# A two-layer hybrid decoder: attention values in column tiles, key blocks merged by the mask, gelu in one ScalarE function, and the last round's sums

## The chip, the cores and the metric

The kernel runs on one core of one Trainium2 chip. A core has five engines that run side by side, each in its own order: TensorE (PE, matrix products; its weight loads are shown as PEld), VectorE (DVE), ScalarE (ACT), GpSimd (POOL) and SyncE (SP, which issues DMAs). The metric is the device time of one execution in microseconds (us).

## What is computed

The input is x, 256 rows of 2048 float32 numbers; two layers are applied. The reference, cut to what matters here:

```python
for l in range(2):
    h = rms_norm(x, mix_norm[l])
    q, k, v, uv, gate_logits = split(h @ w_in[l])          # 16 q heads, 4 kv heads of 64
    q, k = rope(rms_norm(q)), rope(rms_norm(k))
    branch_a = sliding_window_attention(q, k, v, sinks[l]) @ w_attn_branch[l]
    branch_b = chunked_sgu(gelu(uv), w_spatial[l], ...) @ w_sgu_branch[l]
    gates = sigmoid(gate_logits)
    x = x + (gates[:, :D] * branch_a + gates[:, D:] * branch_b) @ w_out[l]
    h2 = rms_norm(x, ffn_norm[l])
    x = x + (silu(h2 @ w_gate[l]) * (h2 @ w_up[l])) @ w_down[l]
```

Attention works on blocks of 128 positions with a window of 128: a query sees the keys at its own position and at the 127 before it. In the first block these lie in that block alone. In the second block, query i sees the keys 0 to i of its own block and the keys i+1 to 127 of the block before: 128 keys in all. `gelu` is the form with tanh: x/2 times 1 + tanh(0.7978845608 (x + 0.044715 x^3)). The softmax has one more entry per head, the sink, which only adds to its denominator.

## The kernel before

**Products.** Each weight matrix streams from HBM in pieces of 256 rows by 512 columns (`raw`, 512 KB in float32; five buffers). Each piece is split into a high part (`whi`, ScalarE, L244) and a low part (`wlo`, VectorE, L245); the activations are split in the same way (`uh`, `ul`). `add_product` (L332 to L341) makes one product of a piece with 128 rows of activations out of six matmuls of 512 columns: high with high, high with low and low with high, for two halves of 128 weight rows. There are four buffers for split pieces; the split runs four pieces ahead of the product (`W_SPLIT`), the load seven (`W_LOAD`).

**Seven products for eight.** Where two column chunks share their activations (`pair`), the first 512 weight rows (unit `WINO`) are done by a Winograd-Strassen scheme with seven products (P1 to P7) for eight. It needs differences of weight pieces (`sums`, VectorE, L229) and of activations (`sums` at L499, split into `sh` and `sl` at L484 and L485). With `two=True` the second 512 rows are done so as well: one product less, three more weight splits and four more subtractions.

**Order.** PE's order is the order in which the program is written; the other engines are ordered by the compiler's schedule. Each two products advance a slot counter by one step (`tick`, L265 on). `after(n, fn)` puts work n steps later; what falls due in the same step is issued in the order in which it was put in. Each of a layer's stages goes through this list: the input projection in chunks (kv, q 0, q 1, gates, v, u), then the attention branch's projection, the SGU branch's, the output projection, then the gated feed-forward part in three rounds of 4, 4 and 3 chunks (`ROUNDS`), each followed by its part of `w_down` (`hid`).

**Attention.** A chunk c holds 8 query heads of two kv groups. `queries` (L722) puts `scores(t, g)` for block t and group g at steps 17, 22, 27, 32 after q 0 is there, and 29, 34, 39, 44 after q 1. `scores` (L745) makes 4 matmuls, two on rows 0 to 63 of the array and two on rows 64 to 127, of 128 columns for each key block, into two PSUM banks of the pool `at`, which has two (`ps_at`); it adds the mask, takes the maximum, Exp and the denominator. Five steps later `weights` (L778) transposes the probabilities of each key block on PE (bank pool `tr`, two banks) and copies them to `pT`; three steps later `values` (L789) multiplies: `pT` (128 x 128) is the stationary operand, 64 columns of v stream, 4 heads for each key block. VectorE divides by the denominator (`att`, L797). When a chunk is complete `transposed` turns `att` around: VectorE transposes blocks of 32 x 32, SP moves them with 16 DMAs, and ScalarE and VectorE split the result into `uh` and `ul`.

**Gelu.** `half` (L807) copies u or v out of PSUM with half the norm's scale. One and two steps later, for each 128 rows, `gelu` (L814) runs a Square and a Tanh on ScalarE and two operations on VectorE.

**Spatial weights.** `fetch` loads them on SP, POOL masks them; `spatial` (L648), 40 steps into the layer, transposes them on PE through both banks of `tr`, and VectorE copies them to `wsT`.

**Sums of the hidden units.** `hidden` (L976) hands `transposed` the steps `WINO_HID` (7, 8, 17, 18, 19, 20) for the first chunk of each round: two scaled copies, the split, the two halves of the sums, their split.

Of the kernel before, what the change touches and what calls it, by code (L numbers as in the profile page):

```python
# [38 lines left out]
WINO_HID = 7, 8, 17, 18, 19, 20  # L39
W_SPLIT = 4  # L40
# [7 lines left out]
Q_FIRST = 17  # L48
Q_STEP = 5
# [4 lines left out]
GELU_A = 0.044715  # L54
GELU_C = 0.7978845608028654
# [3 lines left out]
def hybrid_trunk(ctx: ExitStack, tc: tile.TileContext, x, mix_norm, w_in, q_norm, k_norm, sinks,  # L59
# [64 lines left out]

    def pair(key, wa, wb, by_unit=False, last_later=False, two=False):
# [34 lines left out]
    plans = []  # L160
    for l in range(DEPTH):
# [8 lines left out]
        plans += [single(("att", l), w) for w in cols_of(w_attn_branch[l], NCH)]  # L170
# [32 lines left out]
    class Stream:  # L203
# [7 lines left out]
        def load(self, upto):  # L211
            while self.asked < min(upto, len(entries)):
                for key, w, h, tag in entries[self.asked]["loads"]:
                    raw = (slot([P, 2, CW], name="raw") if tag == "slot" else
                           wraw.tile([P, 2, CW], F32, tag=tag, name=nm("raw"), bufs=None if tag == "raw" else 1))
                    src = w[2 * h * P:2 * (h + 1) * P, :].rearrange("(k p) n -> p k n", p=P)
                    if self.raws:
                        self.loaded = nc.sync.dma_start(raw, src)
                    else:
                        for i in range(2):  # L220
                            self.loaded = nc.sync.dma_start(raw[:, i:i + 1], src[:, i:i + 1])
                    self.raws[key] = raw
                self.asked += 1
# [330 lines left out]
    for c in range(NCH):  # L554
# [4 lines left out]
    mask = const.tile([P, S], F32, name="mask")  # L559
    nc.gpsimd.memset(mask, 0.0)  # L560
    nc.gpsimd.affine_select(mask[:, :P], mask[:, :P], pattern=[[1, P]], base=0, channel_multiplier=-1,
                            compare_op=ALU.is_gt, fill=-1e30)
    nc.gpsimd.affine_select(mask[:, P:], mask[:, P:], pattern=[[-1, P]], base=0, channel_multiplier=1,
                            compare_op=ALU.is_ge, fill=-1e30)
    cs = const.tile([P, NT, HD // 2], F32, name="cs")
# [97 lines left out]
    def fetch_large(pl):  # L663
        for n, i in ((13, 2), (17, 3), (21, 0), (25, 1)):
            after(n, lambda i=i: pl.fetch(i))
        after(40, pl.spatial)

    class Attention:


        def __init__(self, pl):
            self.pl = pl
            self.qT = [None] * 2
            self.att = [None] * 2
            self.attT = [None] * 2
            self.live = {}
# [38 lines left out]
        def keys(self, kv):  # L715
# [4 lines left out]
            after(K_TURN, lambda: turn(self.kT, kd.rearrange("p t n a d -> p t (n a d)"), nc.sync))  # L720

        def queries(self, c, q):  # L722
            self.rotate(q, NQ // 2, self.pl.rope[0], None)
            self.qT[c] = slot([P, 4, S], name="qT")
            self.att[c] = slot([P, NT, CW], name="att")
            after(Q_TURN, lambda: self.turn_queries(c, q))
            n = Q_FIRST + (4 * Q_STEP - 8) * c
# [17 lines left out]
        def scores(self, t, g):  # L745
            nk = P * (t + 1)
            mk = mask[:, P:] if t == 0 else mask
            snk, nsnk = self.pl.snk, self.pl.nsnk
            pr = slot([P, 2, 2, S], name="pr")
            for j in range(2):  # L750
                pscore = ps_at.tile([P, 2, S], F32, tag="at", name=nm("psc"))
                for i in range(2):
# [5 lines left out]
                nc.vector.tensor_tensor(out=pr[:, :, j, :nk], in0=pscore[:, :, :nk],  # L758
                                        in1=mk.unsqueeze(1).to_broadcast([P, 2, nk]), op=ALU.add)
            pr4 = pr.rearrange("p i j k -> p (i j) k")  # L760
            mx = tiny(4, "mx")
            nc.vector.tensor_reduce(out=mx, in_=pr4[:, :, :nk], axis=AX.X, op=ALU.max)
# [7 lines left out]
            for h in range(4):  # L770
                nc.scalar.activation(pr4[:, h, :nk], pr4[:, h, :nk], AF.Exp, bias=nm_[:, h:h + 1],
# [4 lines left out]
            after(5, lambda: self.weights(t, g, pr4, rd))  # L776

        def weights(self, t, g, pr4, rd):  # L778
            pT = []
            for kb in range(t + 1):  # L780
                pt = ps_tr.tile([P, 4, P], F32, tag="tr", name=nm("ppt"))
                for h in range(4):
                    nc.tensor.transpose(pt[:, h, :], pr4[:, h, kb * P:(kb + 1) * P], ident)  # L783
                pT_ = temp((P, 4, P), "pT")
                nc.scalar.activation(pT_, pt, AF.Copy)
                pT.append(pT_)
            after(3, lambda: self.values(t, g, pT, rd))

        def values(self, t, g, pT, rd):  # L789
            po = ps_at.tile([P, 4, HD], F32, tag="at", name=nm("po"))  # L790
            for h in range(4):
                for kb in range(t + 1):
                    nc.tensor.matmul(po[:, h, :], pT[kb][:, h, :],  # L793
                                     self.kv[:, kb, KVW + g * HD:KVW + (g + 1) * HD],
                                     start=kb == 0, stop=kb == t)
            o = (g % 2) * 256
            nc.vector.tensor_tensor(out=self.att[g // 2][:, t, o:o + 256].rearrange("p (h d) -> p h d", d=HD),  # L797
                                    in0=po, in1=rd.unsqueeze(2).to_broadcast([P, 4, HD]), op=ALU.mult)

    class Spatial:  # L800
# [6 lines left out]
        def half(self, ps, name):  # L807

            dst = slot([P, NT, CW], name=name)
            for t in range(NT):  # L810
                nc.scalar.activation(dst[:, t, :], ps[t], AF.Copy, scale=self.nrm.rh[t])
            return dst

        def gelu(self, dst, t):  # L814

            xh = dst[:, t, :]
            sq = temp(name="sq")
            nc.scalar.activation(sq, xh, AF.Square, scale=2.0)
            nc.vector.scalar_tensor_tensor(out=sq, in0=sq, scalar=1.0 / GELU_A, in1=xh,
                                           op0=ALU.add, op1=ALU.mult)  # L820
            nc.scalar.activation(sq, sq, AF.Tanh, scale=2.0 * GELU_C * GELU_A)
            nc.vector.scalar_tensor_tensor(out=xh, in0=sq, scalar=1.0, in1=xh, op0=ALU.add, op1=ALU.mult)

        def v(self, c, ps):
            self.vt[c] = vt = self.half(ps, "v")
            for t in range(NT):
                after(1 + t, lambda t=t: self.gelu(vt, t))
# [30 lines left out]
        def u(self, c, ps):  # L858
            ut = self.half(ps, "u")
            for t in range(NT):  # L860
                after(1 + t, lambda t=t: self.gelu(ut, t))
# [48 lines left out]
    for l in range(DEPTH):  # L910
# [65 lines left out]
        def hidden(hT, c):  # L976
# [6 lines left out]
            def on_up(up):  # L983
                for t in range(NT):
                    nc.vector.scalar_tensor_tensor(out=hid[:, t, :], in0=up[t], scalar=norm.r[t], in1=hid[:, t, :],
                                                   op0=ALU.mult, op1=ALU.mult)
                pe, soon = c == len(hT) - 1 == 2, c == 3
                after(3 if pe else 1 if soon else 2,
                      lambda: transposed(hT, c, hid, on_pe=pe, wino=WINO_HID if c == WINO else None,
# [53 lines left out]
```

## Time and profile before

| | |
|---|---|
| three runs | 2455.78, 2457.51, 2459.42 us; median 2457.51 |
| the profiled execution | 2457.45 us |
| its span, first to last instruction | 2455.7 us |
| mean granted TensorE clock | 0.999 of full speed |
| q1, the DMA queue of the weight loads | 486.35 MB, 61.0% of 16 engines' span |

A row of instructions by group reads: line of the kernel, engine, operation, what it writes <- what it reads, shape, x count | busy us in total, mean ns of one | idle time of the engine just before, and what ended it. A row of the timeline reads: start, duration, engine, line, operation, names, shape, x count, and in brackets the idle time before it and what ended it. The end of a matmul is modelled, so that matmuls in a row overlap in these rows; their starts tell the pace. A row of the waits reads: engine, what waited <- what it waited for: us in total, times, longest. A row of the windows reads: stretch in us, its length, then busy us (and instructions) of PE, PEld, DVE, ACT, POOL, then PE's granted clock, the DMA share and GB/s.

### The profile page before, as it was taken

The numbers are of one execution on the slowest core, as the hardware profiler recorded it, in microseconds if no ns is written. First come the engines' busy times: TensorE is split into PE (matmuls) and PEld (weight loads), VectorE is DVE, ScalarE is ACT, GpSimd is POOL, SyncE is SP. The second block draws the span as 40 slices with busy tenths as digits, with TensorE's granted clock in tenths as the row PEclk, the third lists the DMA queues.
The fourth block names the chain that finished last, engine by engine and source line by source line (L and its number), as shares of the span: only waits on it lengthen the run. The fifth ranks groups of instructions, "written<-read, shape, count | busy, mean of one in ns | idle before, by whom it ended". The sixth has DMA issues, their size and how long they took to land.

```text
span 2455.7 us, 31363 instructions
## 1 busy us (share of the span) xinstructions
PE 2438.1 (99%) x10968; PEld 2012.6 (82%) x10968; DVE 1999.5 (81%) x2320; ACT 1472.5 (60%) x1842; POOL 315.6 (13%) x592
## 2 busy tenths in 40 slices
PE   9999999999999999999999999999999999999999
PEld 7888888888888888887887888888888888888877
DVE  6798676797978997899877986768878789978996
ACT  5567544576655665566655665545666556655664
POOL 3100002132210111001101000021322101110110
PEclk9999999999999999999999999999999999999999
DMA  9555657576667657665747446675767675667654
GB/s 299 196 187 163 212 198 220 186 236 210 220 217 233 210 176 231 230 203 170 229 155 257 152 157 223 202 215 177 246 202 236 204 245 189 200 209 241 203 179 139
DMA packets 280782, 506.74 MB, mean 206 GB/s; under 512 B 28272, under 2 KB 40144, under 8 KB 280624
## 3 DMA queue, kind: packets, MB, share of 16 engines
q1 hardware_dynamic: 262544, 486.35, 61.0%
q0 software_dynamic: 17760, 18.12, 2.8%
q8 instruction: 86, 1.41, 0.2%
q14 instruction: 72, 0.59, 0.1%
q10 hardware_dynamic: 320, 0.27, 0.0%
HBM read 475.27 MB, written 2.10 MB: 194 GB/s over the span
## 4 chain that ended last, share of the span: by engine, by line
PE 90%; DVE 3%; DMA 3%; SPq 1%; issue 1%; ACT 1%; DVEq 0%; ACTq 0%
PE acc L340 59%; PE acc L341 29%; DMA raw<-in_w_in_dram 2%; DVE wlo L245 2%; SPq L416 1%; ACT whi L244 1%; PE po L793 1%; PE psc L754 0%; PE ppt L783 0%; DVE raw L229 0%; PE psg L871 0%; PE pt L453 0%; DMA raw<-in_w_up_dram 0%; DMA raw<-in_w_down_dram 0%; DVE box L410 0%
## 5 line engine op out<-in xcount | busy, mean ns | idle before, releaser
L244 ACT ACTIVATE whi<-raw 128x1024 fp32r<-128x1024 f32 (+1 forms) x1074 | 1132.0, 1059 | 883.0 <-PE acc L341 623.4
L245 DVE TENSOR_TENSOR wlo<-raw,whi 128x1024 fp32r<-128x1024 f32 (+1 forms) x1075 | 1301.3, 1219 | 399.0 <-ACT whi L244 386.7
L340 PE MATMUL acc<-whi,uh 128*128 128x512 f32 x2994 | 1170.3, 391 | 1.2 <-ACT uh L439 1.2
L340 PE MATMUL acc<-wlo,uh 128*128 128x512 f32 x2994 | 1167.1, 390 | 3.0 <-DVE wlo L245 2.9
L341 PE MATMUL acc<-whi,ul 128*128 128x512 f32 x2994 | 1166.4, 390 | 0.0
L340 PEld LDWEIGHTS acc<-wlo,uh 128*128 128x128 f32 x2994 | 562.6, 188 | 123.2 <-DVE wlo L245 6.0
L340 PEld LDWEIGHTS acc<-whi,uh 128*128 128x128 f32 x2994 | 562.6, 188 | 117.7 <-ACT uh L439 1.4
L341 PEld LDWEIGHTS acc<-whi,ul 128*128 128x128 f32 x2994 | 562.3, 188 | 117.8 <-DVE ul L444 0.5
L416 POOL DMA_DIRECT2D tt<-box x544 | 266.5, 497 | 1697.0 <-ACT whi L244 695.5
L229 DVE TENSOR_TENSOR raw<-raw,raw 128x1024 f32<-128x1024 f32 x236 | 287.8, 1219 | 1.6 <-DMA raw<-in_w_up_dram 0.8
L341 PE MATMUL acc<-whi,sl 128*128 128x512 f32 x472 | 184.0, 390 | 3.2 <-DVE sl L485 3.2
L340 PE MATMUL acc<-whi,sh 128*128 128x512 f32 x472 | 184.8, 392 | 1.7 <-ACT acc L364 1.7
L340 PE MATMUL acc<-wlo,sh 128*128 128x512 f32 x472 | 184.2, 390 | 0.0
L341 PEld LDWEIGHTS acc<-whi,sl 128*128 128x128 f32 x472 | 88.6, 188 | 22.5 <-DVE sl L485 4.0
L340 PEld LDWEIGHTS acc<-whi,sh 128*128 128x128 f32 x472 | 88.6, 188 | 20.9 <-ACT acc L364 2.1
L340 PEld LDWEIGHTS acc<-wlo,sh 128*128 128x128 f32 x472 | 88.7, 188 | 18.0
L366 DVE TENSOR_TENSOR kept<-acc,kept 128x512 f32<-128x512 f32 x94 | 64.3, 684 | 10.1 <-PE acc L341 10.1
L369 ACT ACTIVATE acc<-kept 128x512 f32<-128x512 f32 x94 | 54.9, 586 | 4.3 <-DVE kept L366 4.2
L888 DVE SCALAR_TENSOR_TENSOR xs<-acc,xs 128x512 f32<-128x512 f32 (+1 forms) x66 | 42.0, 668 | 8.4 <-PE acc L341 8.1
L436 DVE TENSOR_TENSOR ul<-tt,uh 128x512 fp32r<-128x512 f32 x52 | 34.0, 684 | 2.9 <-ACT uh L435 2.9
L435 ACT ACTIVATE uh<-tt 128x512 fp32r<-128x512 f32 x52 | 29.8, 618 | 9.4 <-DMA tt<-box 9.4
L312 POOL TENSOR_TENSOR rv<-ve,neg_half 128x4 f32<-128x4 f32 x8 | 11.9, 1486 | 172.9 <-DVE ve L839 159.5
(137 smaller groups left out, 874.8 us busy)
## 6 DMA issues: line engine op xcount, KB each, us to landing
raw<-in_w_in_dram SPq DMA_DIRECT2D x239, 512.0 KB, 4.7
raw<-in_w_gate_dram SPq DMA_DIRECT2D x176, 512.0 KB, 4.4
raw<-in_w_up_dram SPq DMA_DIRECT2D x176, 512.0 KB, 4.9
raw<-in_w_down_dram SPq DMA_DIRECT2D x176, 512.0 KB, 5.0
raw<-in_w_out_dram SPq DMA_DIRECT2D x64, 512.0 KB, 5.0
tt<-box POOLq DMA_DIRECT2D x544, 32.0 KB, 4.2
raw<-in_w_attn_branch_dram SPq DMA_DIRECT2D x32, 512.0 KB, 5.6
raw<-in_w_sgu_branch_dram SPq DMA_DIRECT2D x32, 512.0 KB, 4.4
```

The source lines that it names most:

```text
L229: self.last = nc.vector.tensor_tensor(out=self.raws[d], in0=self.raws[x], in1=self.raws[y], op=ALU.subtract)
L244: self.high = nc.scalar.activation(hi[:, i, :], raw[:, i, :], AF.Copy)
L245: self.last = nc.vector.tensor_tensor(out=lo[:, i, :], in0=raw[:, i, :], in1=hi[:, i, :].bitcast(F32), op=ALU.subtract)
L340: nc.tensor.matmul(ps, a, part[:, kk, :], start=first and kk + n == 0, stop=False, skip_group_check=True)
L341: nc.tensor.matmul(ps, b, hi[:, kk, :], start=False, stop=kk == 1, skip_group_check=True)
L366: nc.vector.tensor_tensor(out=p.kept[:, int(tag == "P7"), :], in0=a[1], in1=p.kept[:, 1, :], op=ALU.add)
L369: nc.scalar.activation(ps, p.kept[:, t, :], AF.Copy)
L416: q.dma_start(dst[j * B:(j + 1) * B, i], box[i * B:(i + 1) * B, j])
L435: nc.scalar.activation(h, s_, AF.Copy)
L436: nc.vector.tensor_tensor(out=l, in0=s_, in1=h.bitcast(F32), op=ALU.subtract)
L793: nc.tensor.matmul(po[:, h, :], pT[kb][:, h, :], self.kv[:, kb, KVW + g * HD:KVW + (g + 1) * HD], start=kb == 0, stop=kb == t)
L888: nc.vector.scalar_tensor_tensor(out=xs[:, t, sl], in0=sums[t][:, i * w:(i + 1) * w], scalar=scale, in1=xs[:, t, sl], op0=ALU.mult, op1=AL ...
```

## The change

1. **Key blocks merged.** For the second block the scores of both key blocks are still made. ScalarE copies those of the own block into `pr`; VectorE's `copy_predicated` overwrites those at k > i with the scores of the block before. Maximum, Exp and denominator then see 128 keys, not 256. `pr` is a 2 KB temporary now.
2. **Probabilities are normalised** (VectorE, 4 steps after the scores), then transposed 7 steps after the scores, one transpose for each head. For the second block VectorE makes a second copy with a causal factor (zero where k > i); v of block 0 is multiplied with the plain probabilities, and v of block 1 minus v of block 0 with the masked ones. That difference is made once a layer.
3. **Values.** v (128 x 64) is the stationary operand; the probabilities of 4 heads (512 columns) stream. The two kv groups of a chunk write partitions 0 to 63 and 64 to 127 of one bank: two column tiles of the array. The result has the layout of the activations' units, so `uh` and `ul` are made from the bank at once, and the transposes, DMAs and copies behind `att` go. Rows of `w_attn_branch` are loaded in the matching order, two DMAs of 64 partitions for each piece. `values(t, c)` runs 10 steps after the block's last scores.
4. **Gelu** is one ScalarE function from PSUM with the norm's scale, for each 128 rows.
5. **Spatial weights** are transposed at step 34, not 40.
6. **The last round's sums** (both layers) use `WINO_END`, 12 to 15 steps for the last four parts.
7. **The last pair** of the last `w_down` part in layer 1 runs with `two=True`, so its second hidden unit gets sums too.

```diff
+WINO_END = 7, 8, 12, 13, 14, 15
-Q_FIRST = 17
-Q_STEP = 5
+W_TURN = 7
+SCORES = (17, 22, 27, 32), (29, 34, 39, 44)
...
+    def rows_of(raw, w, h):
+        if w.shape[0] != QW or not any(w is a for a in by_heads):
+            return [(raw, w[2 * h * P:2 * (h + 1) * P, :].rearrange("(k p) n -> p k n", p=P))]
+        rows = w.rearrange("(c a k d) n -> c a d k n", c=2, a=2, d=HD)
+        k = 2 * (h % 2)
+        return [(raw[a * HD:(a + 1) * HD], rows[h // 2, a, :, k:k + 2]) for a in range(2)]
...
-            plans += [pair(("hid", l, r), c_[j], c_[j + 1], j == 0) for j in range(0, NCH, 2)]
+            plans += [pair(("hid", l, r), c_[j], c_[j + 1], j == 0, two=j > 0 and f1 == NF and l == DEPTH - 1)
+                      for j in range(0, NCH, 2)]
...
-        after(40, pl.spatial)
+        after(34, pl.spatial)
...
+            after(K_TURN, lambda: nc.vector.tensor_tensor(out=kv[:, 0, :KVW], in0=kv[:, 1, KVW:], in1=kv[:, 0, KVW:],
+                                                          op=ALU.subtract))
...
             for t in range(NT):
-                for g in (2 * c, 2 * c + 1):
-                    after(n, lambda t=t, g=g: self.scores(t, g))
-                    n += Q_STEP
-            after(n + 6, lambda: transposed(self.attT, c, self.att[c], queue=nc.sync))
+                for i in range(2):
+                    after(SCORES[c][2 * t + i], lambda t=t, g=2 * c + i: self.scores(t, g))
+                after(SCORES[c][2 * t + 1] + W_TURN + 3, lambda t=t: self.values(t, c))
...
-                nc.vector.tensor_tensor(out=pr[:, :, j, :nk], in0=pscore[:, :, :nk],
-                                        in1=mk.unsqueeze(1).to_broadcast([P, 2, nk]), op=ALU.add)
+                if t == 0:
+                    nc.vector.tensor_tensor(out=pr[:, :, j, :], in0=pscore[:, :, :P], in1=mk, op=ALU.add)
+                else:
+                    nc.scalar.activation(pr[:, :, j, :], pscore[:, :, P:], AF.Copy)
+                    nc.vector.copy_predicated(pr[:, :, j, :], mk.bitcast(mybir.dt.uint32), pscore[:, :, :P])
...
-            after(5, lambda: self.weights(t, g, pr4, rd))
+            after(4, lambda: nc.vector.tensor_tensor(out=pr4, in0=pr4, in1=rd.unsqueeze(2).to_broadcast([P, 4, P]),
+                                                     op=ALU.mult))
+            after(W_TURN, lambda: self.weights(t, g, pr4))
...
+            for h in range(4):
+                nc.tensor.transpose(pt[:, h, :], pr4[:, h, :], ident)
+            nc.scalar.activation(pT[0][:, g % 2], pt, AF.Copy)
+            if t == 1:
+                nc.vector.tensor_tensor(out=pT[1][:, g % 2], in0=pt, in1=causal.unsqueeze(1).to_broadcast([P, 4, P]),
+                                        op=ALU.mult)
+
+        def values(self, t, c):
...
+            po = ps_at.tile([P, 4, P], F32, tag="at", name=nm("po"))
+            pT = self.pT[t, c]
+            for k in range(t + 1):
+                for a in range(2):
+                    v = (1 - k) * KVW + (2 * c + a) * HD
+                    nc.tensor.matmul(po[a * HD:(a + 1) * HD], self.kv[:, 0, v:v + HD], pT[k][:, a],
+                                     start=k == 0, stop=k == t)
+            uh, ul = (x[:, :, t * P:(t + 1) * P] for x in units)
+            nc.scalar.activation(uh, po, AF.Copy)
+            nc.vector.tensor_tensor(out=ul, in0=po, in1=uh.bitcast(F32), op=ALU.subtract)
...
+            last = nc.scalar.activation(dst[:, 1, :], ps[1], AF.Gelu_apprx_tanh, scale=self.nrm.r[1])
+            with tc.issue_after(last.ins):
+                nc.scalar.activation(dst[:, 0, :], ps[0], AF.Gelu_apprx_tanh, scale=self.nrm.r[0])
...
+                if c == WINO:
+                    wino = WINO_HID if len(hT) == 4 else WINO_END
+                elif c == WINO + 1 and len(hT) == 3 and l == DEPTH - 1:
+                    wino = WINO_END
```

More of the change, by code (lines that the diff above doesn't have):

```diff
@@ L746, in scores @@
             nk = P * (t + 1)
[L747 removed]
             snk, nsnk = self.pl.snk, self.pl.nsnk
[L749 removed]
+            pr4 = temp((P, 4, P), "pr")
+            pr = pr4.rearrange("p (i j) k -> p i j k", j=2)
             for j in range(2):
@@ L775, in scores @@
             nc.vector.reciprocal(out=rd, in_=den)
-            after(5, lambda: self.weights(t, g, pr4, rd))
[L778 to L787, printed above, removed]
@@ new lines, in scores, with weights @@
+            after(W_TURN, lambda: self.weights(t, g, pr4))
+        def weights(self, t, g, pr4):
+            if g % 2 == 0:
+                self.pT[t, g // 2] = [slot([P, 2, 4, P], name="pT") for _ in range(t + 1)]
+            pT = self.pT[t, g // 2]
+            pt = ps_tr.tile([P, 4, P], F32, tag="tr", name=nm("ppt"))
+            for h in range(4):
+                nc.tensor.transpose(pt[:, h, :], pr4[:, h, :], ident)
[3 more added lines that the diff above has]
+                                        op=ALU.mult)
@@ L805, in __init__, with gelu, v @@
             self.vt, self.sguT = [None] * 2, [None] * 2
-        def half(self, ps, name):
+        def gelu(self, ps, name):
             dst = slot([P, NT, CW], name=name)
-            for t in range(NT):
[L811 to L827, printed above, removed]
+            last = nc.scalar.activation(dst[:, 1, :], ps[1], AF.Gelu_apprx_tanh, scale=self.nrm.r[1])
+            with tc.issue_after(last.ins):
+                nc.scalar.activation(dst[:, 0, :], ps[0], AF.Gelu_apprx_tanh, scale=self.nrm.r[0])
+            return dst
+        def v(self, c, ps):
+            self.vt[c] = self.gelu(ps, "v")
+            for t in range(NT):
                 after(4 + 3 * t, lambda t=t: self.center(c, t))
@@ L858, in u @@
         def u(self, c, ps):
-            ut = self.half(ps, "u")
-            for t in range(NT):
-                after(1 + t, lambda t=t: self.gelu(ut, t))
+            ut = self.gelu(ps, "u")
             for b in range(2):
```

57 lines of the change are left out of this document (26 added, 31 removed).

## The prediction

> **What bounds the kernel now.** First the head of the page and the chain that ended last.
>
> ```profile
> span 2455.7 us, 31363 instructions
> PE 2438.1 (99%) x10968; PEld 2012.6 (82%) x10968; DVE 1999.5 (81%) x2320; ACT 1472.5 (60%) x1842; POOL 315.6 (13%) x592
> PE 90%; DVE 3%; DMA 3%; SPq 1%; issue 1%; ACT 1%; DVEq 0%; ACTq 0%
> ```
>
> PE is busy throughout, so only what removes matmul time or a PE wait moves the end. The timeline of PE gives its pace.
>
> ```profile
> 299.92 0.39 PE L340 MATMUL acc<-whi,uh 128*128 128x512 f32 x1
> 300.14 0.39 PE L340 MATMUL acc<-wlo,uh 128*128 128x512 f32 x1
> ```
>
> The starts stand 0.227 us apart; 0.39 is an overlapping duration. Six such matmuls are a product (1.36 us); two products are a step of the kernel's slot counter (2.72 us). The 1733 products fill 10398 x 0.227 = 2360 us. The rest is attention work on PE and some PE waits. DVE and ACT count only where PE waits for them.
>
> **The change part by part.**
>
> *Values and transposes.* The groups by shape give the counts (two records for each float32 matmul, one for a transpose):
>
> ```profile
> L793 PE MATMUL po<-kv,pT 128*128 128x64 f32 x192 | 23.1, 270 | 0.0
> L783 PE MATMUL ppt<-ident,pr 128*128 128x128 f32 x96 | 13.8, 280 | 2.4 <-DVE wsT L654 2.4
> ```
>
> The timeline of PE around the two sizes of value groups:
>
> ```profile
> 160.72 1.89 PE L793 MATMUL po<-kv,pT 128*128 128x64 f32 x16
> ...
> 162.91 0.39 PE L340 MATMUL acc<-whi,uh 128*128 128x512 f32 x1
> ...
> 193.36 1.00 PE L793 MATMUL po<-kv,pT 128*128 128x64 f32 x8
> ...
> 194.48 0.39 PE L340 MATMUL acc<-wlo,sh 128*128 128x512 f32 x1
> ```
>
> A group costs PE from its start to the second product matmul behind it, less one interval: 162.91 - 0.23 - 160.72 = 1.96 us for sixteen, 194.48 - 0.23 - 193.36 = 0.89 for eight. With 8 groups of each size that is 22.8 us. What replaces them has 512 moving columns, 64 weight columns, 48 records. Two rows bound it: a plain float32 group and the scores, whose halves sit on two row tiles.
>
> ```profile
> 132.93 1.14 PE L754 MATMUL psc<-kT,qT 64*128 64x256 f32 x8
> 134.00 0.66 PE L783 MATMUL ppt<-ident,pr 128*128 128x128 f32 x4
> ...
> 249.93 1.02 PE L871 MATMUL psg<-v,wsT 128*128 128x256 f32 x4
> ...
> 251.02 0.40 PE L340 MATMUL acc<-wlo,uh 128*128 128x512 f32 x1
> ```
>
> L871's 4 records of 256 columns take 251.02 - 0.23 - 249.93 = 0.86 us, 0.215 each, so 0.427 for 512 columns. Eight score records of 256 columns need 1.07 us (132.93 to 134.00) and not 8 x 0.215 = 1.72: the row tiles run side by side, with about 0.2 us for entering and leaving. If column tiles do the same, a first-block group takes 2 x 0.427 + 0.2 = 1.05 us and a second-block group 4 x 0.427 + 0.2 = 1.9; four of each are 11.8 us, a gain of 11.0. If they run one after the other: 48 x 0.427 + 1.6 = 22.1, a gain of 0.7. I take 11.0, by the nearer row (two tiles, float32). The Trainium skill, TensorE: Matmul & The Clock Gate, Part 3 (packing small matmuls), measured 2.38x for three column tiles, 79% of the ideal; estimated by that, the gain would be 8 us. No run here shows column tiles yet.
>
> Merging the key blocks halves the second block's transposes, 32 fewer. What one costs is seen at another group of eight (timeline of PE):
>
> ```profile
> 465.84 1.03 PE L453 MATMUL pt<-ident,gate 128*128 128x128 f32 x8
> ...
> 466.95 0.40 PE L340 MATMUL acc<-wlo,uh 128*128 128x512 f32 x1
> ```
>
> 466.95 - 0.23 - 465.84 = 0.88 us, 0.11 each: a gain of 3.5. The score matmuls stay.
>
> *The bank that values share with scores.* Values moved from step +8 to the last score step +10: 22 + 7 + 3 = 32 is SCORES[0][3], 34 + 10 = 44 is SCORES[1][3]. So the first block's values fall in the same step as the second block's last scores, and stand ahead of them in the list. Also, in layer 0, q 1 comes 8 steps after q 0, so the second block's values (42) meet c = 1's scores (8 + 34). Pool `at` has two banks: the values take one, the first half of the scores the other, and the second half waits until ScalarE's uh and VectorE's ul have read the values. PE runs in order, so the next products wait behind it. Five meetings in all. Before shows one of this kind:
>
> ```profile
> 1410.22 0.71 PE L754 MATMUL psc<-kT,qT 64*128 64x128 f32 x4
> 1411.64 0.71 PE L754 MATMUL psc<-kT,qT 64*128 64x128 f32 x4 [0.71 <-DVE att L797]
> ```
>
> How long uh and ul take to free a bank shows at the group of transposes quoted above, which the same two operations evict (timelines of ACT and DVE):
>
> ```profile
> 466.04 1.06 ACT L244 ACTIVATE whi<-raw 128x1024 fp32r<-128x1024 f32 x1 [1.66 <-PE acc L341]
> 467.00 1.07 ACT L435 ACTIVATE uh<-pt 128x512 fp32r<-128x512 f32 x2
> ...
> 467.13 1.22 DVE L245 TENSOR_TENSOR wlo<-raw,whi 128x1024 fp32r<-128x1024 f32 x1 [1.21 <-ACT whi L244]
> 468.28 1.28 DVE L436 TENSOR_TENSOR ul<-pt,uh 128x512 fp32r<-128x512 f32 x2
> ```
>
> uh stands behind a weight split, ul behind its wlo; the first bank is free at 468.28 + 0.64, 3.1 us after PE began the group at 465.84. With that, a meeting goes: values to 0.95, first half of the scores alone to 1.8, wait to 3.1, second half to 3.95, against 0.95 + 1.07 = 2.0 unhindered: 1.9 lost, four times. The fifth (128 keys): 3.55 against 2.45, 1.1 lost. Sum 8.8; I take **+9**. Bounds: if uh and ul (0.54 + 0.64) came at once, 1 us each, 5 in all; if the DVE queue ahead is the longest, as at 1410 (values at 1406.95, the DVE reads them at 1411.17), 4 to 5.6 each, up to 28. The 0.7 us of that old wait goes.
>
> *Spatial weights six steps sooner.* Timelines of PE and POOL in layer 1, and the window:
>
> ```profile
> 1341.88 0.72 PE L754 MATMUL psc<-kT,qT 64*128 64x128 f32 x8
> 1345.03 0.66 PE L783 MATMUL ppt<-ident,pr 128*128 128x128 f32 x4 [2.43 <-DVE wsT L654]
> ...
> 1346.50 0.63 PE L340 MATMUL acc<-whi,uh 128*128 128x512 f32 x1
> 1346.93 0.63 PE L340 MATMUL acc<-wlo,uh 128*128 128x512 f32 x1
> ...
> 1307.25 0.64 POOL L615 TENSOR_SCALAR_AFFINE_SELECT wsraw<-wsraw 128x512 f32<-128x512 f32 x1 [11.29 <-DMA wsraw<-in_w_spatial_dram]
> ...
> 1340.00:1360.00 20.00, 17.57 (x86) 14.41 (x85) 16.80 (x32) 12.76 (x23) 0.51 (x1) 0.91 0.55 192
> ```
>
> PE waits 2.43 us for a transpose bank that wsT still holds, and then about seven matmuls stand 0.43 apart at a granted clock of 0.91 in this window: 1.4 more. At step 34 the first transposes are five steps away, so both go: 3.8. The spatial load is no bar: it is masked at 1307.9, 33 us ahead of that place, and six steps are 16.
>
> *Sums sooner.* PE waits twice in the last rounds, once in each layer (the waits, PE's timeline, a window):
>
> ```profile
> PE acc L341 <- DVE sl L485: 3.2, 2, 1.6
> ...
> 1153.22 0.40 PE L340 MATMUL acc<-wlo,sh 128*128 128x512 f32 x1
> 1155.19 0.50 PE L341 MATMUL acc<-whi,sl 128*128 128x512 f32 x1 [1.58 <-DVE sl L485]
> ...
> 2385.36 0.50 PE L340 MATMUL acc<-whi,sh 128*128 128x512 f32 x1 [1.68 <-ACT acc L364]
> ...
> 2340.00:2360.00 20.00, 20.00 (x90) 16.57 (x89) 19.79 (x20) 13.73 (x19) 0.00 (x0) 1.00 0.59 191
> ```
>
> 1155.19 - 1153.22 - 0.23 = 1.74 lost, twice. Five steps (13 us) sooner is enough: 3.5 gained. The four subtractions and sl, some 2.9 us, then meet a DVE that is full (19.79 of 20 us); they can delay wlo by that, less than the lead of whi (below), so nothing more. The wait of 1.7 us for L364 I leave as it is: it hangs on ScalarE's order.
>
> *Last pair doubled.* One product less, 1.4 us. It adds three splits, four subtractions and one more set of sums, some 11 us of DVE.
>
> ```profile
> 2420.00:2440.00 20.00, 20.00 (x90) 16.57 (x89) 15.04 (x16) 10.93 (x12) 0.00 (x0) 1.00 0.52 172
> ```
>
> With 5 us free in 20 and 80 us to spread over it just fits: 0, up to 3 if it does not.
>
> *Gelu.* Off go, for each of 16 halves, a Square, a Tanh and two DVE operations; the copy becomes the gelu. Before has four table loads in all. Now three of a layer's four gelu chunks have Exp on both sides (two loads each), the fourth on one: seven more a layer, 14.
>
> ```profile
> L821 ACT ACTIVATE sq<-sq 128x512 f32<-128x512 f32 x16 | 9.8, 619 | 1.5 <-DVE sq L819 1.5
> L822 DVE SCALAR_TENSOR_TENSOR u<-sq,u 128x512 f32<-128x512 f32 x8 | 5.5, 684 | 0.0
> L771 ACT ACT_TABLE_LOAD x1 | 1.3, 1283 | 0.0
> ACT whi L244 <- PE acc L341: 623.4, 573, 4.4
> L340 PE MATMUL acc<-wlo,uh 128*128 128x512 f32 x2994 | 1167.1, 390 | 3.0 <-DVE wlo L245 2.9
> ```
>
> ACT loses 16 x 2 x 0.62 = 20 us and gains 14 x 1.28 = 18; DVE loses 32 x 0.68 = 22. The cover is the split's lead: whi waits 623 us for PE to free a buffer, so it is early, by up to three entries (8 us) less whi and wlo (2.3). A load and two gelus take 2.6. I cost it at nothing; uncovered, 18; and as PE waits only 2.9 us for wlo in all, DVE's relief gains no more than that. The Trainium skill (ScalarE: Activation LUTs, What ACT_TABLE_LOAD costs, and Table sets) says to batch by table set and counts 2.66 us for a switch, 1.28 of load and 1.38 of drain: estimated by that, 37 us of ACT. The load agrees (1283 ns); no drain shows in this trace.
>
> *Off the path.* The old output transposes and 64 box DMAs on SP go. Attention's 32 weight loads become 64 halves on SP, in a stage after the scores whose raw buffers are asked for five entries (13 us) ahead: nothing, by that cover. copy_predicated, which before does not have, is taken as the mask's add that it replaces (VectorE, half the columns); it, the normalisation and the subtraction have three or more steps (8 us) before PE needs them, so twice that duration would cost nothing either.
>
> **Sum**, against the profiled execution's 2457.45 (span plus 1.75; 0.06 under the median shown): -11.0 - 3.5 - 1.4 - 3.5 - 3.8 - 0.7 + 9 = -14.9, so 2442.5 us.
>
> **The rivals.**
>
> (A) Column tiles run one after the other: 10.3 less gained, 2452.8. For it: nothing shows column tiles. Against it: the row tiles.
>
> (B) The bank waits cost little, or another order of ScalarE frees L364 too: 2432 to 2436.
>
> (C) Slower: the bank wait at the five meetings. It decides from 14.9 + 9 + 5 = 29 us, 5.8 each: 4.2 behind a full DVE queue as at 1410, with the half pace of 1346 behind it (1.4). Then about 2463. For it: DVE is the fuller of the two engines; against it: gelu leaves DVE 22 us.
>
> (D) The table loads reach PE: -14.9 + 18 gives 2460.5. For it: they stand in front of splits; against it: the lead above. By the skill's 2.66 us it would be 2479.5.
>
> **How the numbers follow.** Forecast 0.54, A 0.17, B 0.09, C 0.11, D 0.09. About 0.2% (4.9 us) is what a measurement can tell from no change. Forecast and B are faster; A half so, half the same; C slower; D three fifths the same, the rest slower: faster 0.71, same 0.14, slower 0.15. The range goes from B's low end to D's, 2432 to 2460.
>
> **What would show it.** Value groups of 8 records in 1.9 us and not 3.6; 64 transposes; second halves of scores starting 1 to 2 us after the first, released by ul, five times; no PE wait on wsT or sl; 10392 product matmuls; some 14 more table loads and no PE wait behind them. It is wrong if value records stand 0.43 apart, if a bank wait exceeds 3 us, or if PE waits for wlo in attention or in the last pair.

## The result and the profile after

The changed kernel takes 2478.53 us (median; 2477.32 to 2480.79). The kernel before took 2458.48 us beside it. The ratio is 1.0079, with a 95% interval of 1.0070 to 1.0089. The change is slower by 20 us (0.8%), where the forecast was 15 us faster. One execution of the kernel pool_not_doubled below ran at a granted clock of 0.555 and took 4104 us; it is left out of that kernel's median.

The head of the page after: the span, the engines' busy time, and the chain that ended last.

```profile
span 2475.6 us, 30957 instructions
PE 2439.9 (99%) x10786; PEld 2000.5 (81%) x10786; DVE 1990.9 (80%) x2301; ACT 1473.0 (60%) x1839; POOL 315.5 (13%) x593
...
PE 90%; DVE 4%; issue 2%; ACT 2%; DMA 1%; SPq 0%; POOL 0%; DVEq 0%; ACTq 0%
```

PE still bounds the kernel. It runs 182 fewer matmul records and is busy 1.8 us longer. ACT's total is the same to 0.5 us: the table loads eat what the gelu gave back.

The waits of PE after (what waited <- for what: us in total, times, longest):

```profile
PE psc L763 <- DVE ul L817: 14.4, 4, 7.3
PE acc L349 <- DVE wlo L254: 3.4, 5, 1.0
PE acc L349 <- ACT acc L373: 3.3, 1, 3.3
PE acc L350 <- DVE ul L494: 2.3, 1, 2.3
PE psc L763 <- DVE pr L769: 2.2, 1, 2.2
PE acc L350 <- DVE sl L494: 2.0, 1, 2.0
```

The old waits for wsT and att are gone. In their place stand the scores' second halves, which wait for the values' eviction (14.4, and 2.2 released by the scores' own eviction), and three waits of the last rounds. The first meeting on PE, DVE and ACT (L813 are the values, L763 the scores):

```profile
147.84 1.08 PE L813 MATMUL po<-pT,kv 128*64 128x512 f32 x4
148.84 1.13 PE L763 MATMUL psc<-kT,qT 64*128 64x256 f32 x4
157.29 2.07 PE L763 MATMUL psc<-kT,qT 64*128 64x256 f32 x4 [7.31 <-DVE ul L817]
159.29 0.79 PE L349 MATMUL acc<-whi,sh 128*128 128x512 f32 x1
159.88 0.63 PE L349 MATMUL acc<-wlo,sh 128*128 128x512 f32 x1
160.30 0.63 PE L350 MATMUL acc<-whi,sl 128*128 128x512 f32 x1
```

```profile
152.29 0.67 DVE L788 TENSOR_TENSOR pr<-pr,rd 128x512 f32<-128x512 f32 x1
152.88 1.22 DVE L254 TENSOR_TENSOR wlo<-raw,whi 128x1024 fp32r<-128x1024 f32 x1
154.02 0.37 DVE L847 BATCH_NORM_AGGREGATE mv<-bst 128x2 f32<-128x6 f32 x4
154.31 1.19 DVE L254 TENSOR_TENSOR wlo<-raw,whi 128x1024 fp32r<-128x1024 f32 x1
155.42 1.22 DVE L238 TENSOR_TENSOR raw<-raw,raw 128x1024 f32<-128x1024 f32 x1
156.55 0.68 DVE L817 TENSOR_TENSOR ul<-po,uh 128x512 fp32r<-128x512 f32 x1
```

```profile
151.68 1.06 ACT L253 ACTIVATE whi<-raw 128x1024 fp32r<-128x1024 f32 x1 [2.03 <-DVE raw L238]
152.65 0.58 ACT L816 ACTIVATE uh<-po 128x512 fp32r<-128x512 f32 x1
```

The values are done by 148.9. ACT reads their bank only at 152.65, behind a weight split that waited for DVE. DVE reads it at 156.55, behind the normalisation, two splits, a subtraction and the gelu branch's statistics: 8.7 us from the start of the values to ul, against the 2.4 us (465.84 to 468.28) of the model that the prediction took. After the wait the products' starts stand 0.43 us apart.

From the starts of all matmuls in the traces (each matmul's time is the distance to the next one's start) PE's time splits as follows, in us. The last two columns are kernels from the experiments.

| | before | after | v_other_pool | pool_copies_not_doubled |
|---|---|---|---|---|
| scores, with their waits | 17.8 | 37.9 | 13.8 | 13.8 |
| transposes of probabilities | 9.9 | 5.7 | 7.1 | 7.1 |
| values | 20.2 | 11.5 | 11.5 | 11.5 |
| product matmuls | 10398 | 10392 | 10392 | 10398 |
| their time beyond 0.2266 us each | 24.3 | 38.4 | 35.8 | 28.3 |
| span | 2455.7 | 2475.6 | 2450.4 | 2444.5 |

A wait counts to the matmul before it, so the scores of before hold the 2.4 us of waiting for wsT, and the transposes of v_other_pool a wait of 1.2 us that the next product has.

Before to after: +20.1 - 4.2 - 8.7 - 1.4 (six matmuls) + 14.1 = 19.9, the difference of the spans.

### The profile page after: what moved, and what is told of

It is laid out like the page before. It is cut to its first block, busy times and chain, and to the rows that moved or that the text cites. A ratio compares the mean times of both kernels' runs of the same rounds, so it can differ in the third digit from the quotient of the medians.

```text
span 2475.6 us, 30957 instructions
## 1 busy us (share of the span) xinstructions
PE 2439.9 (99%) x10786; PEld 2000.5 (81%) x10786; DVE 1990.9 (80%) x2301; ACT 1473.0 (60%) x1839; POOL 315.5 (13%) x593
## 4 chain that ended last, share of the span: by engine, by line
PE 90%; DVE 4%; issue 2%; ACT 2%; DMA 1%; SPq 0%; POOL 0%; DVEq 0%; ACTq 0%
PE acc L349 59%; PE acc L350 29%; DVE wlo L254 2%; DMA raw<-in_w_in_dram 1%; ACT whi L253 1%; DVE raw L238 1%; PE psc L763 1%; SPq L425 0%; PE pt L462 0%; PE psg L880 0%; DMA raw<-in_w_up_dram 0%; DMA raw<-in_w_down_dram 0%; PE po L813 0%; ACT pr L783 0%; PE ppt L798 0%
## 5 line engine op out<-in xcount | busy, mean ns | idle before, releaser
L349 PE MATMUL acc<-whi,sh 128*128 128x512 f32 x480 | 189.8, 395 | 3.3 <-ACT acc L373 3.3
L349 PE MATMUL acc<-wlo,sh 128*128 128x512 f32 x480 | 189.3, 394 | 0.9 <-DVE kept L375 0.9
L375 DVE TENSOR_TENSOR kept<-acc,kept 128x512 f32<-128x512 f32 x94 | 64.3, 684 | 13.1 <-PE acc L350 13.1
L763 PE MATMUL psc<-kT,qT 64*128 64x128 f32 (+1 forms) x128 | 22.4, 371 | 16.6 <-DVE ul L817 14.4
L763 PEld LDWEIGHTS psc<-kT,qT 64*128 64x128 f32 x128 | 14.2, 197 | 27.2 <-DVE ul L817 16.0
```

The source lines that it names most:

```text
L349: nc.tensor.matmul(ps, a, part[:, kk, :], start=first and kk + n == 0, stop=False, skip_group_check=True)
L375: nc.vector.tensor_tensor(out=p.kept[:, int(tag == "P7"), :], in0=a[1], in1=p.kept[:, 1, :], op=ALU.add)
L763: nc.tensor.matmul(pscore[:, i, :nk], self.qT[pair // 4][j * HD:(j + 1) * HD, pair % 4, t * P:(t + 1) * P], self.kT[j * HD:(j + 1) * HD, : ...
```

## The experiments

Theory: the loss is the bank meetings of values and scores, with the clock's half pace behind them. Rivals: the table loads, and the last rounds' sums. "Before" was 2458 to 2459 us beside every run; as the runs were taken at different times, a difference between two of their medians is good to about 1 us.

**v_two_later** gives the values a step of their own:

```diff
-                after(SCORES[c][2 * t + 1] + W_TURN + 3, lambda t=t: self.values(t, c))
+                after(SCORES[c][2 * t + 1] + W_TURN + 5, lambda t=t: self.values(t, c))
```

> The changed kernel, with the values two steps later, 12 steps after the block's last scores and not 10, so that no score shares their step. Bank theory (the second half of the scores waits for the bank that the values took): the five PE waits on ul go, and the half pace behind them; the score group falls from 37.9 us of PE's time to about 18, the products lose some 7 us less, 2452 us. Table theory (the added table loads hold up the weight splits): the loads stay, 2478 us. Sums theory (the last rounds' order): unchanged, 2478 us.

**v_other_pool** keeps their step and takes the bank from the transposes' pool:

```diff
-            po = ps_at.tile([P, 4, P], F32, tag="at", name=nm("po"))
+            po = ps_tr.tile([P, 4, P], F32, tag="tr", name=nm("po"))
```

> The changed kernel, with the values' bank taken from the transposes' pool tr and not from at; their step stays that of the scores. Bank theory: the waits on ul go as with a later step, 2452 us, perhaps a wait of transposes in their place. If it is not the bank but the step that hurts (a full VectorE or ScalarE there), the products wait for wlo in its place and the time stays near 2478 us. Table and sums theories: 2478 us.

Measured: 2453.28 us (ratio to before 0.9974, 0.9964 to 0.9985) and 2452.17 us (0.9970, 0.9958 to 0.9983). Moving the step or the bank takes 25.2 or 26.4 us off the changed kernel and turns it into a small gain. PE's waits in v_other_pool:

```profile
PE acc L349 <- DVE kept L375: 4.0, 3, 1.9
PE acc L349 <- DVE wlo L254: 3.4, 6, 1.0
PE acc L349 <- ACT acc L373: 3.3, 1, 3.3
```

No score waits any more. A smaller wait has grown: 4.0 us for `kept` (L375) in place of 0.9. The 3.1 that are new lie at 159.7 and 165.9 us, in the stretch from 150 to 166 us in which DVE is busy throughout (16.0 of 16 us).

**one_reader** leaves step and pool as in the changed kernel, but lets the bank be read once:

```diff
-            nc.scalar.activation(uh, po, AF.Copy)
-            nc.vector.tensor_tensor(out=ul, in0=po, in1=uh.bitcast(F32), op=ALU.subtract)
+            out = temp((P, 4, P), "out")
+            nc.scalar.activation(out, po, AF.Copy)
+            nc.scalar.activation(uh, out, AF.Copy)
+            nc.vector.tensor_tensor(out=ul, in0=out, in1=uh.bitcast(F32), op=ALU.subtract)
```

> The changed kernel (2478.5 us), values in their own step and pool, but the bank of values is read once: ScalarE copies it to a temporary, and uh (ScalarE) and ul (VectorE) are made from that. The bank is then free when ScalarE has read it and does not wait for VectorE. In the changed kernel ScalarE's read stood at 152.65 us and VectorE's at 156.55 at the first meeting, and 1.4 us apart at the fourth. If VectorE's queue is what made the meetings cost more than the prediction's 9 us, the 14.4 us of waits for ul fall to 6 to 9 (then for the copy on ScalarE), the first to about 3.5, and the time to about 2469 us. If the bank is held just as long by ScalarE's queue (table loads, two gelus and a split ahead of it), the waits stay at 12 or more and the time within 3 us of 2478.

Measured: 2467.94 us (1.0042, 1.0028 to 1.0056), 10.6 us under the changed kernel. Its waits at the meetings, and the first and the last of them on PE, with ACT and DVE at the first:

```profile
PE psc L763 <- ACT out L817: 5.9, 3, 3.3
```

```profile
153.10 2.07 PE L763 MATMUL psc<-kT,qT 64*128 64x256 f32 x4 [3.30 <-ACT out L817]
...
1456.19 1.92 PE L763 MATMUL psc<-kT,qT 64*128 64x256 f32 x8
```

```profile
152.47 0.58 ACT L817 ACTIVATE out<-po 128x512 f32<-128x512 f32 x1
```

```profile
156.70 0.68 DVE L819 TENSOR_TENSOR ul<-out,uh 128x512 fp32r<-128x512 f32 x1
```

ACT's read and DVE's ul stand within 0.2 us of where they stood; only PE no longer waits for the second. So of the 7.31 us at this place 4.0 were DVE's queue and 3.3 ACT's. All five meetings together: 5.9 us of waits in place of 16.6. The rest of the price is ACT's queue, the half pace behind the waits that are left, and one thing more: the two halves of the scores no longer run side by side. At the last meeting (1456.19) no wait shows and the clock is at 1.00 (1456 to 1458 us), yet the eight records take 1.85 us from their start to the next matmul's, where in v_other_pool they take 1.07: the second half began when the first was done. One wait of 3.5 us came up elsewhere (a transpose for DVE's `ve`).

**gelu_as_before** puts the old gelu (copy, Square, Tanh, two DVE operations) back into the changed kernel:

```diff
...
-            ut = self.gelu(ps, "u")
+            ut = self.half(ps, "u")
+            for t in range(NT):
+                after(1 + t, lambda t=t: self.gelu(ut, t))
```

> The changed kernel with the old gelu (a copy, Square, Tanh and two VectorE operations for each half); the table loads fall from 18 to 4. Table theory: 18 us less, 2460 us. Bank theory: the loads are covered and nothing goes, 2478 us; as VectorE has 22 us more to do, the five bank waits may grow by about 1 us each, up to 2484 us.

Measured: 2474.37 us (1.0060, 1.0045 to 1.0075), 4.2 under the changed kernel, with 4 table loads in place of 18. Where the 4 us are, its waits show, and its first meeting on ACT and PE (L818 and L819 are the changed kernel's L816 and L817):

```profile
PE psc L765 <- DVE ul L819: 10.4, 4, 4.4
```

```profile
148.15 0.60 ACT L818 ACTIVATE uh<-po 128x512 fp32r<-128x512 f32 x1
```

```profile
153.56 2.07 PE L765 MATMUL psc<-kT,qT 64*128 64x256 f32 x4 [4.42 <-DVE ul L819]
```

The waits at the meetings got shorter by 4.0 us, the first from 7.31 to 4.42. Neither expectation was met: the loads are not the cause of the loss (2460 was expected then), but the time fell all the same. The 2.9 us at the first meeting are not a table load's: none stands near it in the changed kernel (the nearest on ACT begin at 130.86 and 169.27 us). With the old gelu both engines' queues are ordered otherwise, and uh comes 1.2 us after the values' start and not 4.8. Only at the fourth meeting does a load stand ahead of uh in the changed kernel, and there the wait is 0.6 us shorter without it:

```profile
1392.20 1.28 ACT L831 ACT_TABLE_LOAD   x1
...
1396.12 0.59 ACT L816 ACTIVATE uh<-po 128x512 fp32r<-128x512 f32 x1
```

**sums_as_before** undoes parts 6 and 7 in the changed kernel:

```diff
-            plans += [pair(("hid", l, r), c_[j], c_[j + 1], j == 0, two=j > 0 and f1 == NF and l == DEPTH - 1)
+            plans += [pair(("hid", l, r), c_[j], c_[j + 1], j == 0)
                       for j in range(0, NCH, 2)]
...
-                wino = None
-                if c == WINO:
-                    wino = WINO_HID if len(hT) == 4 else WINO_END
-                elif c == WINO + 1 and len(hT) == 3 and l == DEPTH - 1:
-                    wino = WINO_END
+                wino = WINO_HID if c == WINO else None
```

> The changed kernel with the last round's sums at the old steps and the last pair not doubled (parts 6 and 7 of the change undone). The prediction's step said that these two parts gain 4.9 us, so undoing them gives 2483 us. Sums theory (they took one wait off and brought another: ScalarE's copies behind splits, sl and ul of the doubled pair): the waits of before return, 6 us in place of 11.8, less the product: 2474 us. Bank theory: no part in it.

Measured: 2474.44 us (1.0060, 1.0045 to 1.0075). The two parts, for which the prediction had a gain of 4.9 us, cost about 4 (4.1 by the medians).

**pool_sums_before** is v_other_pool with the same undone, **pool_sums_gelu_before** has the old gelu as well, and **pool_not_doubled** is v_other_pool without part 7 alone.

> Values in the bank pool of the transposes (measured 2452.2 us), with parts 6 and 7 (the last round's sums sooner, the last pair doubled) undone. In the theory that these two parts cost PE more than they remove (undoing them in the changed kernel itself gave 4 us), the time falls to about 2448 us, the wait for sl comes back (3 us) and the wait for the kept copy L373 in layer 0 goes. In the prediction's terms (a gain of 3.5 and of 1.4) it would rise to about 2457 us. If the two parts only exchange waits, it stays at 2452.

> The kernel of pool_sums_before, with the old gelu (a copy, Square, Tanh and two VectorE operations; 4 table loads in place of 18). Here no bank meeting is left in which a table load can stand, so the price of the new gelu by itself shows. If the 4 us that the old gelu gave in the changed kernel were the table load ahead of uh at the meetings, the old gelu gives nothing here: within 2 us of pool_sums_before, about 2448 us or a little slower, for the two more ScalarE and VectorE operations of each half. If table loads reach PE elsewhere too, it falls by 4 us or more, to 2444 or less.

> Values in the bank pool of the transposes (2452.2 us), with part 7 alone undone: the sums stay sooner, the last pair runs with four products for each half again. The doubled pair saves one product (1.4 us) and its trace shows waits of about 3 us for L494 and L485 in layer 1. If these waits outweigh the product: about 2451 us. If the doubling pays as the prediction has it: 2453.6. Either way the wait for L373 in layer 0 stays (3.3 us), since it belongs to part 6; if it goes, that is wrong.

Measured: 2449.60 (0.9963, 0.9949 to 0.9976), 2450.29 (0.9969, 0.9956 to 0.9981) and 2451.82 us (0.9972, 0.9963 to 0.9981). Without meetings the old gelu gives nothing: in the whole trace of pool_sums_before, with its 18 loads, PE waits 2.3 us for ACT. Parts 6 and 7 cost 2.6 us in this surrounding, at the edge of what these runs resolve; the doubling by itself gives nothing either way (2451.82 against 2452.17). Layer 0's last round in pool_sums_before on PE:

```profile
1154.14 0.50 PE L350 MATMUL acc<-whi,sl 128*128 128x512 f32 x1 [1.58 <-DVE sl L494]
...
1162.47 0.50 PE L349 MATMUL acc<-whi,sh 128*128 128x512 f32 x1 [1.68 <-ACT acc L373]
```

The same round in pool_not_doubled, with the sums sooner, on PE and ACT:

```profile
1164.57 0.80 PE L349 MATMUL acc<-whi,sh 128*128 128x512 f32 x1 [3.33 <-ACT acc L373]
```

```profile
1161.32 1.06 ACT L253 ACTIVATE whi<-raw 128x1024 fp32r<-128x1024 f32 x1 [1.66 <-PE acc L350]
1162.29 1.13 ACT L444 ACTIVATE uh<-tt 128x512 fp32r<-128x512 f32 x2
1163.33 0.57 ACT L372 ACTIVATE kept<-acc 128x512 f32<-128x512 f32 x1
1163.93 0.58 ACT L373 ACTIVATE acc<-acc 128x512 f32<-128x512 f32 x1
```

PE saves the wait for sl and is that much too early for the next thing: P5's copies, which on ACT stand behind a split that waits for PE. 1.6 + 1.7 us became 3.3 in one piece, and after this longer one the products run at half pace (the row at 1176.40 further down shows it for the changed kernel). In pool_not_doubled both layers show it.

**pool_copies_first** takes v_other_pool and makes the first weight split after P5 of the last rounds stand behind P5's copies on ACT:

```diff
-            nc.scalar.activation(a[0], a[1], AF.Copy)
+            copied = nc.scalar.activation(a[0], a[1], AF.Copy)
+            if p.key[0] == "hid" and p.key[2] == 2:
+                stream.copied = copied
...
+                            with tc.issue_after(self.copied.ins):
+                                self.high = nc.scalar.activation(hi[:, i, :], raw[:, i, :], AF.Copy)
+                            self.copied = None
```

> Values in the bank pool of the transposes (2452.2 us), and in the last round of each layer the first weight split behind P5 has to stand behind P5's two kept copies (L372, L373) on ScalarE. In the theory that PE's wait of 3.3 us in layer 0 comes from ScalarE's order (copies queued behind splits that wait for PE), this wait goes and with it the half pace behind it: some 6 us, to about 2446 us. If the copies are late for another reason (the two uh that still stand ahead of them wait for their transposed blocks), the wait stays and so does the time, 2452; and if the splits are what PE then waits for, PE shows waits for whi or wlo in the last round, and the time is 2452 or more.

**pool_copies_not_doubled** is that without the doubled pair.

> Values in the bank pool of the transposes, the last round's sums sooner, the kept copies forced ahead of the next split in both last rounds, and the last pair not doubled (the kernel without the forced copies: 2452.1 us, with two waits of 3.3 us for L373 and a half pace behind each). If the sums' gain was undone by the next deadline alone, P5's kept copies on ScalarE, both waits and both half paces go (5.2 us in layer 0 when it was tried, 4 in layer 1): about 2443 us, the lowest of all. If the wait for sl in layer 1 that came up with the doubled pair (3.7 us) belongs to the forced order and not to the doubling, it shows here again, and the time is about 2447 to 2450 us.

Measured: 2449.81 (0.9965, 0.9952 to 0.9977) and 2446.47 us (0.9950, 0.9937 to 0.9964). Of the first, the half in layer 0 came out as expected, while in layer 1 a wait of 3.7 us for sl took the place; without the doubling that wait does not show, so it belongs to the doubled pair, which costs some 3 us here. The expected 2443 was missed by some 3 us, and waits for wlo grew by as much (6.6 us in all, against 3.4 in pool_not_doubled). PE and ACT in layer 0 of the last kernel (L379 is the changed kernel's L373):

```profile
1159.97 0.49 PE L355 MATMUL acc<-whi,sh 128*128 128x512 f32 x1
```

```profile
1158.73 0.58 ACT L378 ACTIVATE kept<-acc 128x512 f32<-128x512 f32 x1
1159.34 0.58 ACT L379 ACTIVATE acc<-acc 128x512 f32<-128x512 f32 x1
1159.83 1.05 ACT L258 ACTIVATE whi<-raw 128x1024 fp32r<-128x1024 f32 x1
```

The copies come first, and no wait stands in brackets at 1159.97. This kernel beats before by 11.7 us (2458.15 beside it) and the changed kernel by 32.

**pool_spatial_40** is v_other_pool with part 5 undone:

```diff
-        after(34, pl.spatial)
+        after(40, pl.spatial)
```

> Values in the bank pool of the transposes (2452.2 us), with part 5 undone: the spatial weights are transposed at step 40 again. The first transposes now stand at 36 (29 + 7) and the next at 41 and not at 34 and 39. By the prediction's step (the wait for wsT of 2.4 us and the half pace behind it, 3.8 together) the time rises to about 2456 us and a wait for wsT of 2 to 3 us is back in layer 1. If the wait went because the transposes moved, the time stays at 2452 and no such wait shows.

Measured: 2453.87 us (0.9979, 0.9970 to 0.9988), no wait for wsT. Not resolved from v_other_pool's 2452.17. PE in layer 1:

```profile
1345.86 1.03 PE L663 MATMUL pw<-ident,wsraw 128*128 128x128 f32 x8
...
1346.83 0.72 PE L763 MATMUL psc<-kT,qT 64*128 64x128 f32 x8
...
1353.06 0.60 PE L798 MATMUL ppt<-ident,pr 128*128 128x128 f32 x4
```

So part 5 was not needed for the wait to go. The next transposes of probabilities come 7 us behind the spatial ones; their move by two steps is the likely reason, but no run moves it back.

## Why the prediction was wrong

**The step that failed is the price of the bank meetings.** The five meetings were found in their places, and they wait for what the prediction named. The term was +9; taking the meetings away gives 25 to 26. By the matmul starts of the changed kernel, the scores at the five places take 24.1 us more than without values beside them (9.4, 3.3, 3.0, 5.6 and 2.9). Of this 16.6 are waits, where the prediction's model comes to about 6. The other 7.5 are halves that run one after the other, some at half pace, where the model has about 3. Behind them, the products in the 9 us after each place take 8.9 us more than 0.2266 us each; for this half pace the forecast had nothing, though rival C counted it. Taking the meetings away gives less than these 33 us, in part since PE then waits there for other things (4.0 us for wlo and `kept` from 155 to 166 us in v_other_pool).

The model of 467 us was a moment at which ACT and DVE had just caught up: 2.4 us from the start of the transposes to ul. From the start of the values to ul it took 8.7, 4.6, 3.3, 5.0 and 3.0 us at the five places. So the model was near at two of them and far off at the first, where DVE had no idle time for 9 us, and at the fourth, where a table load, two gelus, a split and a copy stand ahead of uh on ACT. The bound of 28 was right and the value was at the wrong end. The row at 1410, from the same stage, was the nearer one for the long waits. Rival C named this and set its price at 5.8 each; 5.0 to 5.3 came out.

**Sums sooner and the doubled pair: -4.9 predicted, +4.1 measured in the changed kernel.** The step "the wait of 1.7 us for L364 I leave as it is" failed. In layer 0 before, a wait of 1.58 us for sl showed and none for that copy; after, sl is in time and PE waits 3.33 us for the copy (L373), with the half pace behind it. The two pool_copies kernels show that ACT's order makes this wait: with the copies first it goes. In layer 1 the 1.58 for sl and 1.68 for the copy gave way to the doubled pair's waits of 2.3 for ul and 2.0 for sl, more than the 1.4 of its product; its bound of 3 allowed for that. These two failures, +16.7 and +9.0, make up 26 of the 35 us between -14.9 and +20.0.

**Values: column tiles do run side by side.** A group of eight after, and what follows it on PE:

```profile
191.17 1.94 PE L813 MATMUL po<-pT,kv 128*64 128x512 f32 x8
193.04 0.71 PE L763 MATMUL psc<-kT,qT 64*128 64x128 f32 x4
```

Eight records of 512 columns take 1.87 us from start to start and four take 1.0, 11.5 in all, against the 11.8 of the forecast. The gain is 8.7, not 11.0, since the old groups cost 20.2 and not 22.8: I had measured them up to the second matmul behind, which adds 0.1 us to each, and the group of sixteen that I took was the slowest of its eight (1.85 us, the others 1.70). Rival A is out.

**Transposes and spatial weights.** The transposes take 4.2 us less (forecast 3.5), and the 2.4 us of waiting for wsT are gone, with the half pace behind it. The cause named was not needed, though: pool_spatial_40 has no such wait without part 5.

**Gelu at nothing: right where no one waits for ACT.** There are 14 more loads, as counted. Rival D's 18 us is out. The 4 us in the changed kernel are waits at the meetings, most of them at one where no load stands, and not a further term.

**Left open.** Without meetings and without parts 6 and 7 the change gives 9.4 us, where the prediction's remaining terms add up to 19.0. Values (2.3) and the waits for `kept`, which before does not have (4.0, of which 3.1 around 160 us), account for two thirds of it. That the latter come from DVE being full there, since the attention change put a copy and a normalisation on it, is argued from the windows and was not tried.

## What to carry to other kernels

Before giving two users of one small bank pool the same step, price the wait by the longest queue that the evicting engines have in that very stretch, not by a typical eviction: at the first meeting the bank was held 9 us by 1.3 us of work. Add what follows a wait, the half pace and the halves that no longer overlap: here that was about as much again. Letting one engine copy the bank out gave back 10.6 us, another pool or another step 25 to 26. When a wait on a saturated engine is removed, find the next deadline on its path first: here waits of 1.6 and 1.7 us in a row became one of 3.3.

## What the runs showed of the hardware

The windows after: PE busy, PEld, DVE, ACT, POOL, then the granted clock.

```profile
148.00:157.00 9.00, 1.97 (x8) 0.70 (x6) 9.00 (x19) 3.47 (x6) 0.00 (x0) 0.71 0.18 55
157.29:162.00 4.71, 4.71 (x10) 3.31 (x11) 2.85 (x10) 1.17 (x6) 1.01 (x1) 0.50 0.69 220
...
1176.40:1182.00 5.60, 5.57 (x13) 4.42 (x14) 3.35 (x5) 1.11 (x2) 0.00 (x0) 0.50 0.59 187
...
1465.00:1469.00 4.00, 3.99 (x11) 2.92 (x12) 1.76 (x5) 0.38 (x1) 0.00 (x0) 0.61 0.78 270
2415.60:2420.00 4.40, 4.38 (x22) 3.68 (x23) 4.33 (x5) 1.43 (x2) 0.00 (x0) 1.00 0.98 337
```

The granted clock falls to one half in or after some waits and stays there for 3 to 6 us of work: to 162.0 after 7.31 us (157.29), to 1182.6 after 3.33 (1176.4), and from 1465.9 to 1469.3 after 1.63 us in a meeting (0.61 is the mean from 1465.0 on). A wait of 2.34 us between full products (2415.6) leaves it at 1.00. The wait's length alone does not decide; the meetings have small matmuls on half of the rows around their waits, and whether that is the reason, or the moment at which a wait falls, was not tried. The Trainium skill (TensorE: Matmul & The Clock Gate, Part 1) puts the drop after an idle window of about 3.4 us. The trace agrees for the wait of 7.31 us, and nearly for that of 3.33; the row at 1465 shows a drop after a shorter one.

One after the other, at the 0.43 us for 512 columns that L871 gives before, four value records would take 1.72 us and eight 3.44. They took 1.0 and 1.87: two column tiles in float32 ran 1.7 and 1.8 times as fast. VectorE's copy_predicated, which before does not have, takes 438 ns where the mask's add of the same shape takes 416:

```profile
L769 DVE TENSOR_TENSOR pr<-psc,mask x16: 409/416/425, 106.6 to 1430.6; 128x256 f32<-128x256 f32 x16
...
L772 DVE COPY_PREDICATED pr<-mask,psc x16: 428/438/449, 137.4 to 1466.7; 128x256 f32<-128x256 uint32 x16
```
